# A weight sum made by an adding DMA in a Strassen-Winograd kernel: one core of Trainium2

## Chip, cores and metric

The kernel runs on one core of one Trainium2 chip. The metric is the device time of one launch in microseconds (us). TensorE is called PE, VectorE DVE, ScalarE ACT, GpSimd POOL and SyncE SP, as in the profile.

## What is computed

The reference is a decoder trunk of two layers on a sequence of 512 tokens with 1024 channels. Per layer:

```
x += 0.5 * g1 * SwiGLU1(rms(x) * (1 + s1) + b1)
x += g2 * Mixer(rms(x) * (1 + s2) + b2)
x += 0.5 * g3 * SwiGLU2(rms(x) * (1 + s3) + b3)

def _swiglu(h, w_gate, w_up, w_down):
    return (jax.nn.silu(h @ w_gate) * (h @ w_up)) @ w_down
```

The factors g, s and b come from a conditioning vector `c` by a product with `ada` weights and a bias `ada_b`. The mixer has one input projection, attention with dilated windows, a short convolution, and two gates, sigmoid(g_conv) and sigmoid(g_attn). All data are float32.

## The kernel before

Activations are held transposed, channels on the 128 partitions. Each float32 operand of PE is split into a high part (`hh`, or the first of a pair in `slots_r`, made by ACT as a cast) and a low part (made by DVE as the difference, helper `sub` on L153); a product is three matmuls, high by high, high by low and low by high.

The FFN's gate and up products and the mixer's gate products are made by groups of seven, class `Seven`, by the scheme of Strassen and Winograd. A group takes two weight tiles of 1024 x 256 as `raw1` and `raw2` (gate and up, or two column blocks of `w_in`), each cut into an upper and a lower half of 512 rows: `a`, `c` from the first, `b`, `d` from the second. It multiplies the 2 x 2 blocks of these weights with the 2 x 2 blocks of the activations in seven products of 24 matmuls (128 x 256), with four sums of activation blocks (`Sums.make`, made once per run of groups) and four sums of weight blocks (`minus` on L581, DVE, 128 x 1024 elements each). Product 5 needs b - a, product 6 needs d - b + a, product 7 needs d - b, and product 4 needs c less the operand of product 6. There are 47 groups: 9 in the first FFN, 10 in each of the three others, and 4 in each layer's mixer. `split5` to `split43` prepare the operands, `run56`, `run7` and `run43` issue the matmuls. `kept` (L577) copies a bank to SBUF on ACT, `plus` (L584) adds a bank on DVE.

Weights are loaded by `load` (L202) on SP's queue, in pieces of 512 KB or 1 MB. A scheduler of the framework decides the order of each engine's instructions; every engine takes its own in order. POOL has little to do: a part of the sums of squares of each norm (`Norm.add`, L402), a power for the reciprocal square root (`rstd_of`, L357), and small copies in the attention.

At the kernel's start, `rows` (L280) reads small tables (norm weights, then `ada_b` of each layer) as rows, by DMAs on ACT's queue (L286), and PE transposes them (L291) into `vec`. The first products of the first FFN (L1429) need `hh`, and this needs the conditioning factors and `rs` of the norm, which PE broadcasts (L1386). The four engines share the rest by lines: L548 and L518 are ACT's casts of weight operands and of activation sums, L315 is DVE's product with the `ada` weights.

Of the kernel before, what the change touches and what calls it, by code (L numbers as in the profile page):

```python
# [120 lines left out]
def trunk(ctx: ExitStack, tc: tile.TileContext, x, c, ada_t, ada_b, norm_g, ffn_w_gate, ffn_w_up, ffn_w_down,  # L124
          w_in, conv_w, w_conv_out, w_attn_out, w_o, rel_bias, final_g, buckets, out):
    nc = tc.nc
    V, A, T, G = nc.vector, nc.scalar, nc.tensor, nc.gpsimd
# [3 lines left out]
    sp = ctx.enter_context(tc.tile_pool(name="sp", bufs=2))  # L131
# [20 lines left out]
    def sub(out_, a, b):  # L152
        V.tensor_tensor(out_, a, b, op=ALU.subtract)  # L153
# [42 lines left out]
    def load(*srcs):  # L196

        raw = wp.tile([P, 8, 2 * P], F32, tag="raw", bufs=RAWS, name="raw")
        col = 0
        for s in srcs:  # L200
            kc, n = s.shape[0] // P, s.shape[1]
            nc.sync.dma_start(raw[:, :kc, col:col + n], s.rearrange("(k p) m -> p k m", p=P))  # L202
            col += n
        return raw

    class Unit:

# [28 lines left out]
    def halves_of(raw, kc):  # L236
        return [Unit(raw, kc, 0), Unit(raw, kc, P)]
# [42 lines left out]

    def rows(srcs, col):
        n = sum(s.shape[0] for s in srcs)
        st = sp.tile([P, P], F32, tag="rows", bufs=2, name="rows")
        at = 0
        for s in srcs:
            nc.scalar.dma_start(st[at:at + s.shape[0]], s)  # L286
            at += s.shape[0]

        def end():
            pt = bank("at")  # L290
            T.transpose(pt[:, :n], st[:n], ident[:n, :n])  # L291
            V.tensor_copy(vec[:, col:col + n], pt[:, :n])

        return end
# [204 lines left out]
    class Sums:  # L499
# [11 lines left out]
        def make(self, i, blocks_):  # L511

            h11, h21, h12, h22 = blocks_
            dst, a, b, op = ((h22, h21, h22, ALU.add), (h22, h22, h11, ALU.subtract),
                             (h21, h11, h21, ALU.subtract), (h22, h12, h22, ALU.subtract))[i - 1]
            V.tensor_tensor(dst, a, b, op=op)
            hi, lo = self.parts[i - 1]
            A.copy(hi, dst)  # L518
            sub(lo, dst, f(hi))
# [45 lines left out]
    class Seven:  # L565

        def __init__(self, raw1, raw2, sums, tag="mm"):
            self.a, self.c = raw1[:, :4], raw1[:, 4:]  # L570
            self.b, self.d = raw2[:, :4], raw2[:, 4:]
            self.sums = sums
            self.one, self.two, self.three = bank(tag), bank("at"), None

        def kept(self, src):
            s = F.take()
            A.copy(s.ap, src)  # L577
            return s

        def minus(self, dst, x, y):  # L580
            V.tensor_tensor(dst, x, y, op=ALU.subtract)  # L581

        def plus(self, s, src):
            V.tensor_tensor(s.ap, s.ap, src, op=ALU.add)  # L584
# [11 lines left out]
        def run2(self):  # L596
            self.p2.run()
            self.plus(self.c11, self.two)

        def split5(self, room=None):  # L600
            self.minus(self.a, self.b, self.a)
            self.three = bank("o")
            self.p5 = Product(self.a, self.sums(1), self.three, True, room)

        def split6(self):
            self.minus(self.a, self.d, self.a)
            self.p6 = Product(self.a, self.sums(2), self.one)

        def run56(self):
            self.p5.run()  # L610
            self.p6.run()
            self.c12 = self.kept(self.one)

        def split7(self):
            self.minus(self.b, self.d, self.b)
            self.p7 = Product(self.b, self.sums(3), self.one)

        def run7(self):
# [2 lines left out]
            self.plus(self.c22, self.three)  # L621

        def split43(self):
            self.minus(self.c, self.c, self.a)
            self.p4 = Product(self.c, quarter(1, 1), self.one)
            self.p3 = Product(self.d, self.sums(4), self.three)

# [5 lines left out]
        def out(self):  # L633
            return self.c11, self.c12, self.one, self.c22

    def first_group(raws):

        sums = Sums()
        group = Seven(*raws, sums, "o")
        group.split1()  # L640
        group.split2()
        group.split5(sums.room())
        return group


# [13 lines left out]
    def gate_up(l, i):  # L659

        held = {}

        def raws(m):
            return [load(w[l, i][:, m * P:(m + 2) * P]) for w in (ffn_w_gate, ffn_w_up)]

        def get(m):
            if m not in held:
                g, u = (halves_of(raw, NC) for raw in raws(m))
                held[m], held[m + 1] = (g[0], u[0]), (g[1], u[1])
            return held.pop(m)  # L670

        get.held, get.raws = held, raws
        return get

    def ffn(l, i, get, first, whole):

        acts = {}
        R.top = N_LOW
        group = first_group(get.raws(len(first) + len(first) % 2))

        def swiglu(m, pg, pu):
            t = F.take()
# [8 lines left out]
        def swiglu_pair(m, g1, u1, g2, u2):  # L691

            A.activation(g1.ap, g1.ap, AF.Silu)
            V.tensor_tensor(u1.ap, u1.ap, g1.ap, op=ALU.mult)
            g1.give()
            s = F.take()
            A.activation(s.ap, g2, AF.Silu)
            V.tensor_tensor(u2.ap, u2.ap, s.ap, op=ALU.mult)
            s.give()
            hi, lo = R.take(2), R.take(2)  # L700
            hv, lv = (s.ap.rearrange("p (c n) -> p c n", c=2) for s in (hi, lo))
            for half, t in enumerate((u1, u2)):
                tv = t.ap.rearrange("p (c n) -> p c n", c=2)
                A.copy(hv[:, :, HALF[half]], tv)
                sub(lv[:, :, HALF[half]], tv, f(hv[:, :, HALF[half]]))
                t.give()
            acts[m], acts[m + 1] = zip(hi.apart(), lo.apart())

        wv = whole.ap.rearrange("p (k n) -> p k n", k=NC)
        sums = group.sums  # L710
# [10 lines left out]
        groups = {len(first) + len(first) % 2: group}  # L721
# [6 lines left out]
        def up(part):  # L728
            modulating["phase"] = "up"
            late = None  # L730
            for m in range(*part):
                if m not in groups:
                    continue
                here, after = groups.pop(m), None
                if not begun[0]:
                    make(1)
                    here.split6()
                    make(2)
                    if len(first) % 2 == 0:
                        for n, banks in enumerate(first):  # L740
                            swiglu(n, *banks)
                else:
                    here.split5()
                    here.split6()
                    if late:
                        swiglu_pair(*late)
                if m + 2 < DFF // P:
                    after = groups[m + 2] = Seven(*get.raws(m + 2), sums)
                    after.split1()
                here.run56()  # L750
# [290 lines left out]
    def mixer(l, first):  # L1041
# [123 lines left out]

        def gate_group(col, m):

            return Seven(*(load(w_in[l][:, col + n * P:col + (n + 2) * P]) for n in (m, m + 2)), sums)

        def seven(here, then, make=None):  # L1170

            here.split5(sums.room() if make else None)
            if make:
                make(1)
            here.split6()
            if make:
                make(2)
            if then:
                then.split1()
            here.run56()  # L1180
# [12 lines left out]
            here.run43()  # L1193

            c11, c12, c21, c22 = here.out()
            s = F.take()
            for a, b in ((c11.ap, c11.ap), (s.ap, c21), (c12.ap, c12.ap), (c22.ap, c22.ap)):
                A.activation(a, b, AF.Sigmoid)
            return [(c11, s), (c12, c22)]

        def begin(group):
# [17 lines left out]
        sums = Sums(False)  # L1219
# [20 lines left out]
        here = begin(gate_group(C_GC, 0))  # L1240
# [300 lines left out]
```

## Time and profile before

| | us |
|---|---|
| median of 3 runs | 2647.26 (2643.28 to 2652.77) |
| profiled execution | 2646.32 |
| its span, first to last instruction | 2644.5 |
| PE busy | 2599.9 |
| DVE busy | 1936.0 |
| ACT busy | 1215.4 |
| POOL busy | 207.6 |

The time is that of one core. An engine's busy time counts its own instructions, and an engine waits when an operand, a free buffer or a bank is not there; the profile names what ended each wait. Engines overlap, so the sums of their busy times exceed the span.

### The profile page before, as it was taken

Reading aid. Unit: us, or ns where it says so; the run is one execution under the profiler, and the core shown is the slowest. Engines: PE = TensorE matmul, PEld = TensorE weight load, DVE = VectorE, ACT = ScalarE, POOL = GpSimd, SP = SyncE. Lnnn points to the kernel's source line nnn. Section 1 sums busy time; section 2 is a strip of 40 time slices with the busy share of each in tenths; the row PEclk is TensorE's granted clock in tenths of the full one; section 3 lists DMA queues with packets and bytes.
Section 4 is the critical chain, followed back from the end, with each engine's and each line's share of the span. In section 5 each row is a group of like instructions: output and inputs, shape, how many; then the busy total and the mean of one; then the engine's idle time right before and its main releaser. Section 6 shows DMA issues by size and latency. Waiting matters only on the chain.

```text
span 2644.5 us, 41896 instructions
## 1 busy us (share of the span) xinstructions
PE 2599.9 (98%) x16841; PEld 2362.5 (89%) x16841; DVE 1936.0 (73%) x2971; ACT 1215.4 (46%) x2224; POOL 207.6 (8%) x545
## 2 busy tenths in 40 slices
PE   8999999999999999999999999999999999999998
PEld 6899999888888989999999999988898888999998
DVE  8987775674685778888788777666756957777675
ACT  5454454353353455444554445443344435545443
POOL 0000031011010020000020000321111000200001
PEclk9999999999999999999999999999999999999999
DMA  9543253352323134353424424343433223233321
GB/s 328 191 161 121 67 156 122 113 166 88 120 88 128 62 130 139 133 191 112 144 73 159 152 96 129 118 130 104 151 112 104 96 96 128 65 112 105 104 77 68
DMA packets 285487, 326.52 MB, mean 123 GB/s; under 512 B 8057, under 2 KB 263404, under 8 KB 285292
## 3 DMA queue, kind: packets, MB, share of 16 engines
q1 hardware_dynamic: 284980, 323.71, 37.5%
q8 instruction: 132, 2.16, 0.3%
q14 instruction: 63, 0.52, 0.1%
q10 hardware_dynamic: 312, 0.13, 0.0%
HBM read 321.67 MB, written 2.13 MB: 122 GB/s over the span
## 4 chain that ended last, share of the span: by engine, by line
PE 66%; DVE 2%; ACT 1%; DMA 1%; POOL 0%; issue 0%; POOLq 0%; ACTq 0%; DVEq 0%; SPq 0%
PE mm L559 14%; PE o L559 9%; PE mm L243 8%; PE mm L244 8%; PE mm L245 8%; PE at L559 4%; PE o L243 2%; PE o L245 2%; PE o L244 2%; PE mm L1130 2%; PE at L245 2%; PE at L244 2%; PE at L243 2%; DVE slots_r L153 1%; PE o L967 1%
## 5 line engine op out<-in xcount | busy, mean ns | idle before, releaser
L153 DVE TENSOR_TENSOR slots_r<-raw,slots_r 128x1024 fp32r<-128x1024 f32 (+3 forms) x457 | 447.6, 999 | 148.6 <-ACT slots_r L548 91.7
L548 ACT CAST slots_r<-raw 128x1024 fp32r<-128x1024 f32 x329 | 341.0, 1049 | 445.7 <-DVE raw L581 71.1
L223 DVE TENSOR_TENSOR slots_r<-raw,slots_r 128x512 fp32r<-128x512 f32 (+3 forms) x520 | 320.7, 638 | 211.4 <-ACT slots_r L222 77.2
L222 ACT CAST slots_r<-raw 128x512 fp32r<-128x512 f32 (+3 forms) x520 | 289.7, 577 | 381.5 <-PE mm L245 106.0
L243 PE MATMUL mm<-hh,slots_r 128*128 128x512 f32 (+1 forms) x1064 | 385.2, 365 | 0.0
L244 PE MATMUL mm<-hl,slots_r 128*128 128x512 f32 (+1 forms) x1064 | 383.3, 361 | 0.3 <-DVE hl L153 0.3
L245 PE MATMUL mm<-hh,slots_r 128*128 128x512 f32 (+1 forms) x1064 | 382.6, 360 | 0.0
L559 PE MATMUL o<-slots_r 128*128 128x256 f32 x2448 | 310.6, 285 | 6.1 <-ACT slots_r L518 3.1
L559 PEld LDWEIGHTS o<-slots_r 128*128 128x128 f32 x2448 | 302.6, 193 | 8.2 <-ACT slots_r L518 3.7
L559 PE MATMUL mm<-slots_r 128*128 128x256 f32 x2064 | 264.8, 284 | 2.5 <-ACT slots_r L548 0.9
L559 PE MATMUL mm<-hh,slots_r 128*128 128x256 f32 x1376 | 258.5, 280 | 5.9 <-ACT slots_f L577 5.9
L559 PEld LDWEIGHTS mm<-slots_r 128*128 128x128 f32 x2064 | 255.5, 193 | 5.6 <-ACT slots_f L577 3.1
L581 DVE TENSOR_TENSOR raw<-raw 128x1024 f32<-128x1024 f32 x188 | 230.0, 1226 | 3.9 <-DMA raw<-in_w_in_dram 0.6
L245 PEld LDWEIGHTS mm<-hh,slots_r 128*128 128x128 f32 x1064 | 201.3, 189 | 32.2
L244 PEld LDWEIGHTS mm<-hl,slots_r 128*128 128x128 f32 x1064 | 201.8, 190 | 26.6 <-DVE hl L153 0.6
L559 PEld LDWEIGHTS mm<-hh,slots_r 128*128 128x128 f32 x1376 | 216.4, 188 | 9.4 <-ACT slots_f L577 9.1
L243 PEld LDWEIGHTS mm<-hh,slots_r 128*128 128x128 f32 x1064 | 200.5, 190 | 26.5 <-ACT hh L377 0.2
L244 PE MATMUL mm<-slots_r 128*128 128x512 f32 (+1 forms) x584 | 212.3, 364 | 0.0
L243 PE MATMUL mm<-slots_r 128*128 128x512 f32 (+1 forms) x584 | 212.3, 365 | 0.0
L245 PE MATMUL mm<-slots_r 128*128 128x512 f32 (+1 forms) x584 | 212.2, 363 | 0.0
L559 PE MATMUL mm<-hl,slots_r 128*128 128x256 f32 x688 | 192.0, 279 | 0.0
L559 PE MATMUL at<-hh,slots_r 128*128 128x256 f32 x752 | 141.4, 280 | 0.9 <-DVE slots_r L153 0.9
(197 smaller groups left out, 4598.1 us busy)
## 6 DMA issues: line engine op xcount, KB each, us to landing
slots_f<-in_ada_t_dram SPq DMA_DIRECT2D x144, 512.0 KB, 4.7
raw<-in_w_in_dram SPq DMA_DIRECT2D x52, 1024.0 KB, 5.1
raw<-in_ffn_w_gate_dram SPq DMA_DIRECT2D x42, 1024.0 KB, 5.2
raw<-in_ffn_w_up_dram SPq DMA_DIRECT2D x42, 1024.0 KB, 5.7
raw<-in_ffn_w_down_dram SPq DMA_DIRECT2D x32, 768.0 KB, 4.8
raw<-in_w_in_dram SPq DMA_DIRECT2D x48, 512.0 KB, 5.1
raw<-in_ffn_w_down_dram SPq DMA_DIRECT2D x20, 512.0 KB, 3.4
raw<-in_w_conv_out_dram SPq DMA_DIRECT2D x8, 1024.0 KB, 7.4
```

The costliest lines, as they stand in the source:

```text
L153: V.tensor_tensor(out_, a, b, op=ALU.subtract)
L222: A.copy(hv, src)
L223: (eng or V).tensor_tensor(lv, src, f(hv), op=ALU.subtract)
L243: T.matmul(dst, hi, xh[:, cols], start=first, stop=False)
L244: T.matmul(dst, hi, xl[:, cols], start=False, stop=False)
L245: T.matmul(dst, lo, xh[:, cols], start=False, stop=last)
L548: A.copy(hv, src)
L559: T.matmul(dst, a, b, start=self.first and k == i == n == 0, stop=True, skip_group_check=True)
L581: V.tensor_tensor(dst, x, y, op=ALU.subtract)
L967: T.matmul(dst, a, b, start=first[bk], stop=True, skip_group_check=True)
L1130: T.matmul(dst, a, b, start=k == 0 and r % 2 == 0 and n == 0, stop=True, skip_group_check=True)
```

## The change

Quarter `b` of the second weight tile gets `d` added by a DMA from POOL's queue, which reads the same half of the weights again and adds it to what the load put there. Products take the derived sums with changed signs: `a += b` is the operand of product 6, then `c += a` that of product 4, then `a -= d` that of product 5, and b itself that of product 7. Product 6 is made and run ahead of product 5. The changed signs are taken back in `Sums.make`, in `swiglu_pair` and in the scale of a sigmoid. The tile of `rows` gets one buffer where it had two, and a scratch area for DMAs 4096 bytes where it had 1024.

```diff
-        st = sp.tile([P, P], F32, tag="rows", bufs=2, name="rows")
+        st = sp.tile([P, P], F32, tag="rows", bufs=1, name="rows")
...
-            dst, a, b, op = ((h22, h21, h22, ALU.add), (h22, h22, h11, ALU.subtract),
-                             (h21, h11, h21, ALU.subtract), (h22, h12, h22, ALU.subtract))[i - 1]
-            V.tensor_tensor(dst, a, b, op=op)
+            dst, a, b = ((h22, h22, h21), (h22, h22, h11), (h21, h11, h21), (h22, h22, h12))[i - 1]
+            if i % 2:
+                sub(dst, a, b)
+            else:
+                V.scalar_tensor_tensor(dst, a, -1.0, b, op0=ALU.mult, op1=ALU.subtract)
...
-        def __init__(self, raw1, raw2, sums, tag="mm"):
+        def __init__(self, srcs, sums, tag="mm"):
+
+            raw1, raw2 = (load(s) for s in srcs)
             self.a, self.c = raw1[:, :4], raw1[:, 4:]
             self.b, self.d = raw2[:, :4], raw2[:, 4:]
+            G.dma_start(self.b, srcs[1][D // 2:].rearrange("(k p) m -> p k m", p=P), accum_op=ALU.add)
...
+        def split6(self, room=None):
+            V.tensor_tensor(self.a, self.a, self.b, op=ALU.add)
+            self.p6 = Product(self.a, self.sums(2), self.one, room=room)
+
         def split5(self, room=None):
-            self.minus(self.a, self.b, self.a)
+            V.tensor_tensor(self.c, self.c, self.a, op=ALU.add)
+            sub(self.a, self.a, self.d)
             self.three = bank("o")
             self.p5 = Product(self.a, self.sums(1), self.three, True, room)
 
-        def split6(self):
-            self.minus(self.a, self.d, self.a)
-            self.p6 = Product(self.a, self.sums(2), self.one)
-
-        def run56(self):
-            self.p5.run()
+        def run6(self):
             self.p6.run()
             self.c12 = self.kept(self.one)
 
+        def run5(self):
+            self.p5.run()
+
         def split7(self):
-            self.minus(self.b, self.d, self.b)
             self.p7 = Product(self.b, self.sums(3), self.one)
...
         def split43(self):
-            self.minus(self.c, self.c, self.a)
...
-            V.tensor_tensor(u1.ap, u1.ap, g1.ap, op=ALU.mult)
+            V.scalar_tensor_tensor(u1.ap, u1.ap, -1.0, g1.ap, op0=ALU.mult, op1=ALU.mult)
...
-    nc = bacc.Bacc("TRN2", target_bir_lowering=False, num_devices=1, dynamic_dma_scratch_size=1024)
+    nc = bacc.Bacc("TRN2", target_bir_lowering=False, num_devices=1, dynamic_dma_scratch_size=4096)
```

`split5` and `split6` change places in `ffn`, in `first_group` and in the mixer's `seven`, and `run6` and `run5` follow each other there. In the changed file the lines stand 1 to 7 further down (L286 is L287, L1429 is L1436, the adding DMA is L578).

The first pair of orders is that of ACT at the kernel's start; `rows` is the small table's tile, `in_ada_b_dram` the bias, `slots_f<-slots_f` the activation of `c`. Before:

```order
L286 DMA rows<-in_final_g_dram 8x128
L286 DMA rows<-in_ada_b_dram 72x128
L1367 ACTIVATE hl,ssq<-slots_f 128x1024 x4
L1383 ACTIVATE slots_f<-slots_f 128x1024
L286 DMA rows<-in_ada_b_dram 72x128
L1376 COPY xT<-mm 128x4x128 x4
L1388 COPY slots_f<-at 128x512
```

After:

```order
L287 DMA rows<-in_final_g_dram 8x128
L1374 ACTIVATE hl,ssq<-slots_f 128x1024 x4
L1390 ACTIVATE slots_f<-slots_f 128x1024
L287 DMA rows<-in_ada_b_dram 72x128
L1383 COPY xT<-mm 128x4x128 x4
L287 DMA rows<-in_ada_b_dram 72x128
L1395 COPY slots_f<-at 128x512
```

Both transfers of `ada_b` have moved down, the first behind the five activations, the second behind the four copies.

The second pair is that of DVE at the first group of the mixer's gates in layer 0. `raw_6908` and `raw_6910` are the group's weight tiles; L516 and L519 are `make`, and L153 or L154 with `slots_r` is the lower part of an operand, of a weight block where `raw` is read and of an activation sum where `slots_f` is. Before:

```order
L581 TENSOR_TENSOR raw_6908<-raw_6910,raw_6908 128x1024
L584 TENSOR_TENSOR slots_f_70<-slots_f_70,at_6913 128x512
L516 TENSOR_TENSOR slots_f_70<-slots_f_70 128x1024
L153 TENSOR_TENSOR slots_r_69<-raw_6908,slots_r_69 128x1024
L516 TENSOR_TENSOR slots_f_70<-slots_f_70 128x1024
L153 TENSOR_TENSOR slots_r_69<-raw_6910,slots_r_69 128x1024
L153 TENSOR_TENSOR slots_r_69<-slots_f_70,slots_r_69 128x1024 x2
```

After:

```order
L609 TENSOR_TENSOR raw_6908<-raw_6908 128x1024
L588 TENSOR_TENSOR slots_f_70<-slots_f_70,at_6914 128x512
L154 TENSOR_TENSOR slots_f_70<-slots_f_70 128x1024
L154 TENSOR_TENSOR raw_6908<-raw_6908,raw_6910 128x1024
L154 TENSOR_TENSOR slots_f_70<-slots_f_70 128x1024
L154 TENSOR_TENSOR slots_r_69<-slots_f_70,slots_r_69 128x1024
L154 TENSOR_TENSOR slots_r_69<-raw_6908,slots_r_69 128x1024
L519 SCALAR_TENSOR_TENSOR slots_f_70<-slots_f_70 128x1024
```

The lower parts of product 5's sum and weight have moved ahead of `make(2)`, and one `make` (that of product 7) too.

The third pair is that of POOL from the last attention head of layer 0 to the norm of the second FFN. Before:

```order
L813 COPY ng_6496<-top 32x2 x16
L813 COPY sm0x<-sm_6529 32x2 x16
L402 TENSOR_TENSOR slots_f<-slots_f 128x256 x5
L357 TENSOR_TENSOR rs<-rs,minus_half 128x2
L402 TENSOR_TENSOR slots_f<-slots_f 128x256 x5
```

After:

```order
L819 COPY ng_6496<-top 32x2 x16
L578 DMA raw<-in_w_in_dram 128x4x256
L819 COPY sm0x<-sm_6529 32x2 x16
L578 DMA raw<-in_w_in_dram 128x4x256 x3
L578 DMA raw<-in_ffn_w_up_dram 128x4x256
L403 TENSOR_TENSOR slots_f<-slots_f 128x256 x3
L578 DMA raw<-in_ffn_w_up_dram 128x4x256
L403 TENSOR_TENSOR slots_f<-slots_f 128x256 x2
L358 TENSOR_TENSOR rs<-rs,minus_half 128x2
L403 TENSOR_TENSOR slots_f<-slots_f 128x256 x5
```

Six adding DMAs now stand between POOL's instructions here, one of them within the first five sums of squares.

## Rows read from the trace of the kernel before

**Rows 1.** The page: the span, and PE's busy time, share and instructions.

```profile
span 2644.5 us, 41896 instructions
PE 2599.9 (98%) x16841; PEld 2362.5 (89%) x16841; DVE 1936.0 (73%) x2971; ACT 1215.4 (46%) x2224; POOL 207.6 (8%) x545
```

**Rows 2.** Who waited for whom, PE: us in total, times, longest.

```profile
PE mm L559 <- ACT slots_f L577: 6.6, 5, 1.7
PE at L411 <- POOL slots_f L402: 3.7, 2, 1.9
```

**Rows 3.** Groups of DVE by form: busy us, mean ns | idle before, releasers.

```profile
L581 DVE TENSOR_TENSOR raw<-raw 128x1024 f32<-128x1024 f32 x188 | 230.0, 1226 | 3.9 <-DMA raw<-in_w_in_dram 0.6
...
L388 DVE SCALAR_TENSOR_TENSOR xT<-mm,mod,xT 128x512 f32<-128x512 f32 x72 | 52.1, 744 | 14.1 <-PE mm L245 14.1
...
L694 DVE TENSOR_TENSOR slots_f<-slots_f 128x512 f32<-128x512 f32 x39 | 26.8, 687 | 0.6
```

**Rows 4.** Timeline of DVE in the second FFN: start, duration, instruction, [idle before, releaser].

```profile
1095.99 2.49 DVE L581 TENSOR_TENSOR raw<-raw 128x1024 f32<-128x1024 f32 x2
1098.39 0.68 DVE L584 TENSOR_TENSOR slots_f<-slots_f,o 128x512 f32<-128x512 f32 x1
...
1117.62 1.23 DVE L153 TENSOR_TENSOR slots_r<-raw,slots_r 128x1024 fp32r<-128x1024 f32 x1 [3.70 <-ACT slots_r L548]
```

**Rows 5.** Timeline of PE there: product 3, then the next group's product 5.

```profile
1122.07 5.93 PE L559 MATMUL o<-slots_r 128*128 128x256 f32 x48
```

**Rows 6.** DMA issues: count, KB each, median us from issue to landing.

```profile
raw<-in_w_in_dram SPq DMA_DIRECT2D x48, 512.0 KB, 5.1
raw<-in_ffn_w_down_dram SPq DMA_DIRECT2D x20, 512.0 KB, 3.4
```

**Rows 7.** Timeline of ACT at the start.

```profile
11.13 0.32 ACTq L286 DMA_DIRECT2D rows<-in_ada_b_dram  x1
```

**Rows 8.** Timeline of PE at the start.

```profile
14.78 1.06 PE L1386 MATMUL at<-ident,rs 128*128 128x128 f32 x4
17.57 0.38 PE L291 MATMUL at<-ident,rows 72*128 72x72 f32 x1 [1.72 <-DMA rows<-in_ada_b_dram]
18.27 2.01 PE L1429 MATMUL mm<-hh,slots_r 128*128 128x512 f32 x3 [0.32 <-ACT hh L1401]
...
24.55 0.50 PE L1429 MATMUL o<-hh,slots_r 128*128 128x512 f32 x1 [0.96 <-DVE slots_r L223]
```

**Rows 9.** Stretches: length, busy us (instructions) of PE, PEld, DVE, ACT, POOL; clock; DMA.

```profile
18.00:92.00 74.00, 68.77 (x363) 57.38 (x364) 73.60 (x116) 39.48 (x56) 0.00 (x0) 0.97 0.71 249
...
791.50:796.80 5.30, 5.27 (x24) 5.28 (x25) 5.30 (x6) 1.08 (x2) 0.00 (x0) 0.50 0.01 3
...
2096.00:2103.00 7.00, 5.35 (x26) 4.76 (x27) 7.00 (x9) 2.19 (x4) 0.00 (x0) 0.76 0.00 0
```

**Rows 10.** Timeline of PE at the first mixer group of layer 0.

```profile
789.21 0.38 PE L559 MATMUL o<-slots_r 128*128 128x256 f32 x1 [1.85 <-ACT slots_r L518]
791.53 5.28 PE L559 MATMUL o<-slots_r 128*128 128x256 f32 x23 [1.93 <-DVE slots_r L153]
...
806.75 0.50 PE L559 MATMUL o<-slots_r 128*128 128x256 f32 x2 [1.02 <-ACT slots_r L548]
```

**Rows 11.** SP's timeline in the stretch from 960 to 975 us, the last load.

```profile
963.38 0.37 SPq L202 DMA_DIRECT2D raw<-in_ffn_w_up_dram  x1
```

**Rows 12.** DMA issues of that stretch: the same load, us to landing.

```profile
raw<-in_ffn_w_up_dram SPq DMA_DIRECT2D x1, 1024.0 KB, 7.2
```

**Rows 13.** Timeline of POOL at the norm of the second FFN.

```profile
969.24 3.19 POOL L402 TENSOR_TENSOR slots_f<-slots_f 128x256 f32<-128x256 f32 x4 [2.07 <-ACT slots_f L399]
974.67 0.71 POOL L357 TENSOR_TENSOR rs<-rs,minus_half 128x2 f32<-128x2 f32 x1 [2.24 <-DVE rs L356]
...
977.83 0.74 POOL L402 TENSOR_TENSOR slots_f<-slots_f 128x256 f32<-128x256 f32 x1 [1.57 <-ACT slots_f L399]
```

**Rows 14.** Timeline of PE there.

```profile
982.08 0.39 PE L244 MATMUL mm<-hl,slots_r 128*128 128x256 f32 x1 [0.35 <-DVE hl L153]
```

More of the change, by code (lines that the diff above doesn't have):

```diff
@@ L578, in kept @@
             return s
-        def minus(self, dst, x, y):
-            V.tensor_tensor(dst, x, y, op=ALU.subtract)
         def plus(self, s, src):
@@ L634, in out, with first_group @@
             return self.c11, self.c12, self.one, self.c22
-    def first_group(raws):
+    def first_group(srcs):
         sums = Sums()
-        group = Seven(*raws, sums, "o")
+        group = Seven(srcs, sums, "o")
         group.split1()
         group.split2()
-        group.split5(sums.room())
+        group.split6(sums.room())
         return group
@@ L661, in gate_up, with srcs @@
         held = {}
-        def raws(m):
-            return [load(w[l, i][:, m * P:(m + 2) * P]) for w in (ffn_w_gate, ffn_w_up)]
+        def srcs(m):
+            return [w[l, i][:, m * P:(m + 2) * P] for w in (ffn_w_gate, ffn_w_up)]
         def get(m):
             if m not in held:
-                g, u = (halves_of(raw, NC) for raw in raws(m))
+                g, u = (halves_of(load(s), NC) for s in srcs(m))
                 held[m], held[m + 1] = (g[0], u[0]), (g[1], u[1])
             return held.pop(m)
-        get.held, get.raws = held, raws
+        get.held, get.srcs = held, srcs
         return get
@@ L678, in ffn @@
         R.top = N_LOW
-        group = first_group(get.raws(len(first) + len(first) % 2))
+        group = first_group(get.srcs(len(first) + len(first) % 2))
         def swiglu(m, pg, pu):
@@ L697, in swiglu_pair @@
             A.activation(s.ap, g2, AF.Silu)
-            V.tensor_tensor(u2.ap, u2.ap, s.ap, op=ALU.mult)
+            V.scalar_tensor_tensor(u2.ap, u2.ap, -1.0, s.ap, op0=ALU.mult, op1=ALU.mult)
             s.give()
@@ L736, in up @@
                     make(1)
-                    here.split6()
+                    here.split5()
                     make(2)
@@ L742, in up @@
                 else:
+                    here.split6()
                     here.split5()
-                    here.split6()
                     if late:
@@ L747, in up @@
                 if m + 2 < DFF // P:
-                    after = groups[m + 2] = Seven(*get.raws(m + 2), sums)
+                    after = groups[m + 2] = Seven(get.srcs(m + 2), sums)
                     after.split1()
-                here.run56()
+                here.run6()
+                here.run5()
                 make(3)
@@ L1166, in gate_group @@
         def gate_group(col, m):
-            return Seven(*(load(w_in[l][:, col + n * P:col + (n + 2) * P]) for n in (m, m + 2)), sums)
+            return Seven([w_in[l][:, col + n * P:col + (n + 2) * P] for n in (m, m + 2)], sums)
         def seven(here, then, make=None):
-            here.split5(sums.room() if make else None)
+            here.split6(sums.room() if make else None)
             if make:
                 make(1)
-            here.split6()
+            here.split5()
             if make:
@@ L1179, in seven @@
                 then.split1()
-            here.run56()
+            here.run6()
+            here.run5()
             if make:
@@ L1196, in seven @@
             s = F.take()
-            for a, b in ((c11.ap, c11.ap), (s.ap, c21), (c12.ap, c12.ap), (c22.ap, c22.ap)):
-                A.activation(a, b, AF.Sigmoid)
+            for a, b, sign in ((c11.ap, c11.ap, 1.0), (s.ap, c21, 1.0), (c12.ap, c12.ap, -1.0), (c22.ap, c22.ap, -1.0)):
+                A.activation(a, b, AF.Sigmoid, scale=sign)
             return [(c11, s), (c12, c22)]
```

## The prediction

> **What bounds the kernel now.** I read the page's totals first, then the waits of TensorE (PE), then the stretches where these waits lie. PE is busy for 2599.9 of 2644.5 us [rows 1]: all its gaps together are 44.6 us, and that is the most that any change can win which leaves PE's matmuls as they are. This one does: every group still has seven products of 24 matmuls, in the order 6, 5, 7 where it was 5, 6, 7. VectorE (DVE), which loses work, is no bound over the whole, so what counts is where PE waits for it. The largest waits tell where [rows 2]. Those for the copy on L577 are 6.6 us, nearly all of them one wait of about 1.6 us in the last group of each FFN, where product 4 needs the bank that `kept` still copies; product 7, that copy and product 4 follow each other as before, so they stay. The waits for GpSimd's (POOL) sums of squares are 3.7 us. The rest lies at the kernel's start and at the first group of each run of groups, and is shown below.
>
> **DVE's work.** Four subtractions of 1.226 us per group become three additions or subtractions of the same tile size, so 47 of the 188 go: 47 x 1.226 = 57.6 us [rows 3]. The signs turn some TENSOR_TENSORs into SCALAR_TENSOR_TENSORs; at 512 columns the one form is 0.687 us (L694) and the other 0.744 (L388, which also reads a bank), so 0 to 0.06 us each, on some 80 of 512 columns and 12 of 1024, that is 0 to 6 us of DVE time. Neither is on PE's path inside a run of groups. There DVE works far ahead: its first subtractions on a new group start at 1095.99 [rows 4], by when both weight tiles have landed, and PE reaches the group's product 5 only in the second half of the 48 matmuls from 1122.07 [rows 5], at 1122.07 + 5.93 / 2 = 1125. What covers DVE is thus some 29 us of earlier products, and taking 1.2 us out of that lead is worth **0**.
>
> **The accumulating DMA.** No such transfer is in the trace. It moves 512 KB. Loads of this size from SyncE (SP) land 3.4 and 5.1 us after issue [rows 6]; below I can't go under 3.4, and above I allow 14: twice the 5.1, for reading the destination too, and some 4 for POOL's issue, which no row prices. I take 6, near the plain load. Its wait for the load holds nothing in a run of groups but the next such DMA. Behind it stands `a += b`. In the changed order that addition comes after the addition onto `c22` that starts at 1098.39 and takes 0.68 [rows 4], so at least 3 us of the transfer are hidden before DVE notices, and a blocked DVE then eats into the lead of 29 us; DVE also has slack to catch up, such as the 3.70 us before 1117.62 [rows 4]. I take a third of that lead as free (10 us), a choice, since DVE has the other work of two groups to do in it; then PE stalls only if the transfer takes over 3 + 10 = **13 us** from the load's landing. At 6 us: 0. The Trainium skill, "DMA: Bandwidth & Descriptors", section "Anatomy of one DMA", fits a transfer issued from GpSimd with 2.0 us plus the bytes at 436 GB/s, which makes an estimate of 3.2 us here; by it the sum is the same.
>
> **The kernel's start.** `rows` gets one buffer where it had two, and this I price highest. Before, the first `ada_b` transfer is issued with the other small ones, and only the second at 11.13 [rows 7]; it lands at 17.57, 6.4 us later, in a stretch where loads fill the queue, and PE's transposition of it ends just before the first product (18.27) [rows 8]. After (the first pair of order fences), the first `ada_b` transfer has to wait for PE's transposition of the earlier rows and stands behind the activation of `c`: it is issued at about 11.1 and lands at about 17.6. PE transposes it ahead of the broadcast of `rs` (14.78 before), so everything that hangs on that, `hh` above all, comes 17.95 - 14.78 = 3.2 us later: 18.27 + 3.2 = 21.4. The second can be issued only at about 18.0, and by the same 6.4 us lands at 24.4, and its transposition stands ahead of the first product: PE starts at 24.5 and not at 18.27, 6.2 us late. Some comes back, for PE waited later for DVE and ScalarE (ACT) too (0.96 us before 24.55 [rows 8], and later again), and these are only 3.2 us late. From 18 to 92 us DVE is busy 73.60 of 74.00 us [rows 9]; it is the bound of that stretch, so its 3.2 us reach the end of it whole, less 0.5 for the first group (one 1024-column operation less, one of 512 more ahead of its last sums). The bounds are 0 (the small transfer lands early) and +6.2; I take **+3.5**. In the same stretch the first group's accumulate runs while loads fill the queue: **+0.5**, bounds -1 and +4.
>
> **The first groups of the mixers.** PE waits 1.85 and 1.93 us at 789 and 791 and 1.02 us at 806.75 [rows 10]; at 791.5 the granted clock is 0.50 for 5.3 us, the lower of the two levels (1.2 GHz), in which 24 matmuls take 5.3 us where 24 take 3.0 at 2.4 GHz [rows 5, 9]. So this start costs 2.0 + 1.9 + 2.3 + 1.0 = some 7 us, and that of layer 1 (PE busy 5.35 of 7 us at a clock of 0.76 [rows 9]) 1.7 of waits and as much of clock. DVE decides both. Ahead of the first products one 1.2-us subtraction is gone, and the lower half of the sums of product 5 now comes ahead of `make(2)` (second pair of fences): the second matmul of product 5 can start about 1.1 us earlier, and the later waits shrink by 1 to 2 us. The clock still falls, because PE still waits some 3 us. I take -2.5 and -0.5, together **-3**; bounds -12 (waits and clock all gone) and +1.
>
> **POOL's queue.** Two accumulates stand ahead of or among the sums of squares of each later norm (third pair of fences), and in a queue in order the sums wait for a weight load and the issue. The load that the second one waits for is issued at 963.38 [rows 11] and takes 7.2 us to land [rows 12], at 970.6. POOL's sums run from 969.24, the power at 974.67 [rows 13]: two of them can come some 1 to 2 us later, and the power with them. The sums behind wait for ACT anyway (1.57 us before 977.83 [rows 13]), which takes the delay up. PE waits 0.35 us for `hl` at 982.08 [rows 14], so there is hardly slack. Three such places, 0 to +1.7 each: **+2**, bounds 0 and +5.
>
> **Sum.** 0 + 3.5 + 0.5 - 3 + 2 = +3 on the profiled execution's 2646.3 us (its span of 2644.5 and 1.8 around it), which is 0.9 below the median of the runs: 2649.
>
> **The rivals.** (1) *Nothing shows*: the small transfers at the start land soon and POOL's delays are taken up; what is left is the mixers' -3: 2643 to 2647. For it speaks that every term is small; against, that the row on the load of `ada_b` gives 6.4 us in just that stretch. (2) *Faster*: DVE's relief at the mixers' starts is enough that PE doesn't fall to the lower clock, -12, and the start costs at most +2: 2636. Against it: the table load and casts of ACT are ahead of the same products, and they stay. (3) *Slower by the starts*: all of +6.2, +4 and +5 and no gain at the mixers: 2646 + 15 = 2661. (4) *Slower by the accumulate*: from 13 us on it decides; at 15 each of some 35 groups inside a run loses 2 us: 2646 + 70 = 2716. For it: the transfer has to read its destination too, and no row bounds its issue on POOL; against: DVE's lead. The Trainium skill, "SBUF — State Buffer", section "two separate sides", has a rule that speaks for it: descriptors of a DMA issued on GpSimd are written through a port pair that DVE can lock, and one such DMA went from 0.62 to 3.1 us beside a copy. Times five, 6 us would be 30, and every group would lose 17; but it names copies in a two-port mode, and DVE here does additions and subtractions. No row here shows either. (5) *The change does not do what it says*: the subtractions go as counted, that is sure from the order; it is only the time that can miss.
>
> **Chances.** My forecast (2647 to 2654) 0.45, rival 1 0.20, rival 2 0.11, rival 3 0.16, rival 4 0.08. Measurement tells 0.3%, 7.9 us, from no change: the first two are "same", 0.65; faster 0.11; slower 0.24. The range leaves out rival 4 and most of rival 2: 2639 to 2663.
>
> **What would show it.** Right: 141 operations on the three new lines in DVE; PE's first product at about 24 us; no new waits inside the runs of groups; PE's sum of gaps within 10 us of 44.6; POOL's power near 976. Wrong: waits of PE or DVE for a DMA from GpSimd's queue in every group; a first product still at 18; a clock of 1.0 at the mixers' start.

## The result, and the profile after

The changed kernel takes 2685.1 us, median of 4 runs (2678.7 to 2695.9), beside 2649.8 for the kernel before (4 runs): a ratio of 1.0135, with a 95% interval of 1.0114 to 1.0157. It is 35 us slower where I forecast no measurable change.

The page of the kernel after, span and busy times:

```profile
span 2685.9 us, 42026 instructions
PE 2612.6 (97%) x16841; PEld 2372.1 (88%) x16841; DVE 1881.1 (70%) x2924; ACT 1209.2 (45%) x2224; POOL 267.1 (10%) x592
```

Against [rows 1] DVE has 54.9 us less work, about what was counted, and PE has the same 16841 matmuls. PE's gaps are now 2685.9 - 2612.6 = 73.3 us where they were 44.6, which is 28.7 us more. The other 12.7 us of the 41.4 us by which the span grew are PE's own: the same matmuls are busy longer. The mean granted clock of the run is 0.989 where it was 0.993, so some 0.011 x 2685.9 = 29.5 us are lost to the clock where 18.5 were: 11 of the 12.7. One such fall stands right behind a wait of 3.66 us that is shown below (stretch: length, busy us of PE, PEld, DVE, ACT, POOL; clock; DMA):

```profile
1342.00:1348.00 6.00, 6.00 (x29) 6.00 (x29) 1.62 (x6) 1.71 (x4) 1.44 (x2) 0.50 0.00 0
```

At this place the kernel before had a clock of 0.75 for 6 us. So a gap can be paid partly a second time, in the matmuls behind it.

Who waited for whom on PE, after (us in total, times, longest):

```profile
PE mm L562 <- ACT slots_f L584: 9.8, 9, 2.5
PE at L412 <- POOL slots_f L403: 9.3, 5, 3.7
PE at L292 <- DMA rows<-in_ada_b_dram: 7.7, 2, 5.1
PE o L562 <- DVE slots_f L588: 7.1, 6, 2.1
...
PE o L562 <- ACT slots_r L551: 4.6, 4, 2.2
```

No releaser in this list is the adding DMA. The two rows of [rows 2] have grown to 9.8 and 9.3 us, and the third row, the small table at the start, is new in its size. The DMA shows one engine further back. First DVE's groups by form (busy us, mean ns | idle before, releasers), then the adding DMA's issues in the FFNs (min/median/max ns on POOL, first and last start), and the us to landing of all 47:

```profile
L605 DVE TENSOR_TENSOR raw<-raw 128x1024 f32<-128x1024 f32 x47 | 57.5, 1224 | 75.9 <-issue 36.6 <-DMA raw<-in_ffn_w_up_dram 33.0 <-DMA raw<-in_w_in_dram 3.1
L154 DVE TENSOR_TENSOR raw<-raw 128x1024 f32<-128x1024 f32 x47 | 57.5, 1223 | 1.0
L609 DVE TENSOR_TENSOR raw<-raw 128x1024 f32<-128x1024 f32 x47 | 57.5, 1223 | 0.7
```

```profile
L578 POOL DMA_DIRECT2D raw<-in_ffn_w_up_dram x39: 1273/1288/1465, 60.1 to 2589.0; - x39
...
DMA to landing us min/median/max: 5.6/5.8/9.2
```

DVE stands 75.9 us in all before the 47 additions `a += b` (L605), and hardly at all before the other two of each group (1.7 us). The profile names no releaser for 36.6 of the 75.9 us (`issue`). The landings tell: in 26 of the 47 groups the addition starts 0.08 us after its adding DMA has landed, and these groups have some 73 of the 75.9 us. The transfer itself is what I had assumed: 5.8 us, and 1.29 us of POOL for its issue.

**Where the time goes.** From the start of the matmul with the same number in each trace I worked out how far a kernel lags the kernel before (us; negative is ahead):

| place (time before) | after | e2 | e6 | e8 | e3 |
|---|---|---|---|---|---|
| 214.5, first FFN | 8.4 | 4.3 | 1.9 | 2.2 | 0.1 |
| 811.7, mixer of layer 0 | 7.0 | 1.3 | 2.4 | -1.7 | -3.2 |
| 1258.0, second FFN | 13.6 | 3.4 | 2.5 | -0.6 | -4.5 |
| 1341.6, third FFN begun | 21.6 | 5.6 | 3.0 | 6.7 | -5.5 |
| 1421.3, its `w_down` begun | 29.6 | 6.5 | 6.6 | 8.3 | -3.8 |
| end | 41.0 | 5.7 | 9.5 | 14.2 | -4.5 |

The loss comes in steps. The two largest, of 7 to 8 us, lie where one kind of work passes into another; the others are of 1 to 4 us. The two, in the rows of the kernel after:

*Second FFN to third.* DVE's timeline (start, duration, instruction, [idle before, releaser]), then POOL's and PE's:

```profile
1321.99 1.22 DVE L154 TENSOR_TENSOR slots_r<-raw,slots_r 128x1024 fp32r<-128x1024 f32 x1
1331.40 1.23 DVE L605 TENSOR_TENSOR raw<-raw 128x1024 f32<-128x1024 f32 x1 [8.20 <-issue]
1332.54 0.75 DVE L389 SCALAR_TENSOR_TENSOR xT<-mm,mod,xT 128x512 f32<-128x512 f32 x1
```

```profile
1322.11 1.29 POOL L578 DMA_DIRECT2D raw<-in_ffn_w_up_dram  x1 [61.22 <-DVE xT L389]
...
1337.66 3.93 POOL L403 TENSOR_TENSOR slots_f<-slots_f 128x256 f32<-128x256 f32 x5 [5.22 <-ACT slots_f L400]
```

```profile
1333.43 0.36 PE L244 MATMUL mm<-slots_r 128*128 128x256 f32 x1 [1.60 <-DVE xT L389]
1341.64 2.72 PE L412 MATMUL at<-ones,slots_f 128*128 128x1 f32 x12 [3.66 <-POOL slots_f L403]
```

The adding DMA of the third FFN's first group is issued at 1322.11 and lands 9.2 us later, at 1331.3, the longest of all (SP had issued two weight loads at 1320.50 and 1320.96). DVE has come to `a += b` at 1323.20 and stands until 1331.40. The operand of that addition is needed only after the next norm. But behind it in DVE's queue stand the residual additions of the second FFN (L389), and they are needed at once: by PE for a bank, by ACT and POOL for the next norm, and by PE for its sums. PE's waits of 1.60 and 3.66 us name DVE and POOL, and the cause is a DMA two engines away.

*Last group of the third FFN to `w_down`.* POOL, DVE, SP, ACT and PE, one row or two each, with the same columns:

```profile
1400.35 1.33 POOL L578 DMA_DIRECT2D raw<-in_ffn_w_up_dram  x1 [31.14 <-DMA raw<-in_ffn_w_up_dram]
...
1406.35 1.23 DVE L605 TENSOR_TENSOR raw<-raw 128x1024 f32<-128x1024 f32 x1 [4.26 <-DMA raw<-in_ffn_w_up_dram]
...
1415.27 8.38 SPq L203 DMA_DIRECT2D raw<-in_ffn_w_down_dram  x3
...
1420.05 1.44 ACT L223 CAST slots_r<-raw 128x512 fp32r<-128x512 f32 x3 [5.26 <-DMA raw<-in_ffn_w_down_dram]
1421.40 0.57 ACT L584 COPY slots_f<-mm 128x512 f32<-128x512 f32 x1
...
1422.02 0.39 PE L562 MATMUL mm<-hh,slots_r 128*128 128x256 f32 x1 [2.15 <-ACT slots_f L584]
```

The same loads on SP's queue in the kernel before:

```profile
1389.04 7.56 SPq L202 DMA_DIRECT2D raw<-in_ffn_w_down_dram  x3
```

The lag at this place, at 1377.1 of before, is 22.0 us, so the `w_down` loads would go at 1411.0. They go at 1415.27, 4.2 us later, when DVE has read the group's weight tiles for the last time (L154, from 1414.03 to 1415.25). DVE has stood 4.26 us at the addition that these readings stand behind. ACT's cast then waits 5.26 us for one of these loads, the copy `kept` (L584) stands behind the cast, and PE waits 2.15 us for the copy.

### The profile page after: what moved, and what is told of

Same layout as the page of the kernel before. It is cut to its first block, busy times and chain, and to the rows that moved or that the text cites. A ratio compares the mean times of both kernels' runs of the same rounds, so it can differ in the third digit from the quotient of the medians.

```text
span 2685.9 us, 42026 instructions
## 1 busy us (share of the span) xinstructions
PE 2612.6 (97%) x16841; PEld 2372.1 (88%) x16841; DVE 1881.1 (70%) x2924; ACT 1209.2 (45%) x2224; POOL 267.1 (10%) x592
## 4 chain that ended last, share of the span: by engine, by line
PE 74%; DVE 11%; DMA 8%; ACT 3%; issue 3%; POOL 1%; SPq 0%; POOLq 0%; DVEq 0%; ACTq 0%
PE mm L562 12%; PE mm L245 11%; PE mm L244 11%; PE mm L246 10%; PE o L562 8%; DMA raw<-in_ffn_w_up_dram 4%; DVE slots_r L154 4%; PE mm L1136 3%; PE at L562 2%; PE o L244 2%; PE o L246 2%; PE o L245 2%; DMA raw<-in_ffn_w_down_dram 2%; PE at L246 2%; PE at L245 2%
## 5 line engine op out<-in xcount | busy, mean ns | idle before, releaser
L154 DVE TENSOR_TENSOR slots_r<-raw,slots_r 128x1024 fp32r<-128x1024 f32 (+3 forms) x457 | 446.9, 1003 | 161.9 <-ACT slots_r L551 97.4
L562 PE MATMUL o<-slots_r 128*128 128x256 f32 x2448 | 320.4, 288 | 14.1 <-DVE slots_f L588 7.1
L562 PEld LDWEIGHTS mm<-hh,slots_r 128*128 128x128 f32 x1376 | 217.2, 189 | 14.4 <-ACT slots_f L584 13.2
L578 POOL DMA_DIRECT2D raw<-in_ffn_w_up_dram x39 | 50.5, 1296 | 1302.4 <-DMA raw<-in_ffn_w_up_dram 663.2
```

Source lines behind the costliest of these rows:

```text
L562: T.matmul(dst, a, b, start=self.first and k == i == n == 0, stop=True, skip_group_check=True)
L578: G.dma_start(self.b, srcs[1][D // 2:].rearrange("(k p) m -> p k m", p=P), accum_op=ALU.add)
```

## The experiments

**e2: nobody waits soon for the sum.** `a` gets `d` and not `b` added, so products 6, 4 and 5 take other sums. The DMA stays, and its first reader is the split of product 7.

```diff
-            V.tensor_tensor(self.a, self.a, self.b, op=ALU.add)
+            V.tensor_tensor(self.a, self.a, self.d, op=ALU.add)
```

> The changed kernel with a += d in the place of a += b: DVE's operation has the same size and place, but d is there with the load, so it need not wait for the adding DMA; the DMA still runs, and its sum is first read by product 7. Product 6 and what is derived from it get another weight sum than the reference's. Theory A: 22 to 32 us faster than the changed kernel, at most 10 us above before. Rival B: within 5 us of the changed kernel, since queue and traffic are the same. Rival C: the same as the changed kernel.

Measured: 2655.8 us, 1.0022 [1.0013, 1.0032]. Same DMAs, same number of DVE operations, and 30 of the 36 us (1.0135) are gone. DVE's row in e2 and PE's waits:

```profile
L605 DVE TENSOR_TENSOR raw<-raw 128x1024 f32<-128x1024 f32 x47 | 57.4, 1221 | 1.3 <-DMA raw<-in_ffn_w_up_dram 0.5
```

```profile
PE at L292 <- DMA rows<-in_ada_b_dram: 8.3, 2, 5.4
PE at L412 <- POOL slots_f L403: 7.6, 5, 1.9
...
PE mm L562 <- ACT slots_f L584: 1.3, 3, 0.6
```

So it is the wait at `a += b` that costs these 30 us, not the transfer's traffic or its issue.

**e3: the same order and signs, the sum on DVE.** No adding DMA; `rows` has its two buffers and the scratch area its 1024 bytes again.

```diff
-            G.dma_start(self.b, srcs[1][D // 2:].rearrange("(k p) m -> p k m", p=P), accum_op=ALU.add)
...
+            V.tensor_tensor(self.b, self.b, self.d, op=ALU.add)
```

> No adding DMA: b += d is made on DVE, so each group has four DVE operations as before, but in the order and with the signs of the changed kernel; rows with two buffers and the scratch area of before. Theory A: within 5 us of before (2645 to 2655), or a few us faster. Rival C: still 15 us or more slower than before. Rival B: near before too.

Measured: 2643.8 us, 0.9977 [0.9968, 0.9987]: faster than both kernels. DVE does the 57.7 us of additions that the change had removed, and waits less:

```profile
L604 DVE TENSOR_TENSOR raw<-raw 128x1024 f32<-128x1024 f32 x47 | 57.7, 1228 | 22.6 <-DMA raw<-in_ffn_w_up_dram 11.9 <-DMA raw<-in_w_in_dram 10.7
```

DVE's addition waits for the load alone (22.6 us); through the DMA the same sum is there about 6.5 us after the load (0.7 to the issue, 5.8 to landing) where DVE makes it in 1.2.

**e4: the kernel before with one buffer for `rows`.**

```diff
-        st = sp.tile([P, P], F32, tag="rows", bufs=2, name="rows")
+        st = sp.tile([P, P], F32, tag="rows", bufs=1, name="rows")
```

> The kernel before with one buffer for rows, nothing else. All theories but D: 3 to 6 us slower than before, PE's first product at 24 us and not at 18. Rival D: 25 us or more slower. If the late transfer is hidden: no difference.

Measured: 2648.4 us, 0.9996 [0.9986, 1.0005]. PE's timeline at its start:

```profile
22.92 0.35 PE L291 MATMUL at<-ident,rows 72*128 72x72 f32 x1 [5.50 <-DMA rows<-in_ada_b_dram]
23.02 2.91 PE L1429 MATMUL mm<-hh,slots_r 128*128 128x512 f32 x6
```

The first product is 4.75 us later than in [rows 8], as foreseen, and the time does not show it.

**e5: the changed kernel with two buffers for `rows`**, the scratch area at 2048 bytes, since two buffers and 4096 bytes (e1) don't fit together in SBUF.

```diff
-        st = sp.tile([P, P], F32, tag="rows", bufs=1, name="rows")
+        st = sp.tile([P, P], F32, tag="rows", bufs=2, name="rows")
...
-    nc = bacc.Bacc("TRN2", target_bir_lowering=False, num_devices=1, dynamic_dma_scratch_size=4096)
+    nc = bacc.Bacc("TRN2", target_bir_lowering=False, num_devices=1, dynamic_dma_scratch_size=2048)
```

> The changed kernel with two buffers for rows, the scratch area cut to 2048 bytes so that both fit. Theory A, with the one buffer worth little: within 5 us of the changed kernel (2685), PE's first product back at 18 us. If the start, though nothing in the kernel before, counts where DVE is later anyway: 4 to 8 us faster than the changed kernel. Rival E (the scratch area sets the pace of the adding DMA): slower than the changed kernel.

Measured: 2681.4 us, 1.0127 [1.0112, 1.0142], which overlaps the 1.0135 of the change, with PE's first product back at 18.26. The start is not where the 35 us are. Nor does the smaller scratch area slow the adding DMA: its median to landing is 5.8 us as before.

**e6: the tile that gets the sum is loaded first.** Loads of a group change places, nothing else.

```diff
-            raw1, raw2 = (load(s) for s in srcs)
+            raw2, raw1 = (load(s) for s in srcs[::-1])
```

> The changed kernel with the order of each group's two loads turned round: the tile that is added to is loaded first, so the adding DMA runs while the other tile is loaded. Theory A: DVE's waits at a += b, 73 us in the changed kernel, fall under 20 us, and the time by 20 to 30 us, to 2655 to 2665. Rival B (queue and traffic): within 5 us of the changed kernel.

Measured: 2655.3 us, 1.0019 [1.0008, 1.0031]. The adding DMA now runs beside the load of the other tile, and L605 waits 6.2 us in all:

```profile
L605 DVE TENSOR_TENSOR raw<-raw 128x1024 f32<-128x1024 f32 x47 | 57.4, 1220 | 6.2 <-DMA raw<-in_ffn_w_up_dram 3.6 <-issue 1.2 <-DVE slots_r L154 0.6
```

So the wait can be taken away with the DMA kept.

**e7: e6 with e5's two edits**, the tile loaded first and two buffers for `rows`.

```diff
+            raw2, raw1 = (load(s) for s in srcs[::-1])
...
+        st = sp.tile([P, P], F32, tag="rows", bufs=2, name="rows")
...
+    nc = bacc.Bacc("TRN2", target_bir_lowering=False, num_devices=1, dynamic_dma_scratch_size=2048)
```

> As the run with the turned loads, and two buffers for rows with 2048 bytes of scratch. Theory A: 0 to 4 us faster than the turned loads alone; 2645 to 2662. It is the version that could be as fast as the sum made on DVE (2644) if nothing of the DMA is left on the path.

Measured: 2652.8 us, 1.0018 [1.0008, 1.0027]: no difference from e6 that shows.

**e8: half the sum.** The DMA adds 256 KB into the first two of the four blocks of `b`; the other two get no sum.

```diff
-            G.dma_start(self.b, srcs[1][D // 2:].rearrange("(k p) m -> p k m", p=P), accum_op=ALU.add)
+            G.dma_start(self.b[:, :2], srcs[1][D // 2:D // 2 + 2 * P].rearrange("(k p) m -> p k m", p=P), accum_op=ALU.add)
```

> The changed kernel with an adding DMA of half the rows (256 KB; the lower two of four blocks of b get no sum). Theory A: the DMA lands some 1 to 2 us sooner, each of some 23 waits at a += b is shorter by that, and the time falls by 8 to 16 us, to 2669 to 2677. Rival C (order and signs): the same as the changed kernel. Rival B: some 5 us faster.

Measured: 2661.5 us, 1.0047 [1.0031, 1.0063]. DVE's row, and the landing:

```profile
L605 DVE TENSOR_TENSOR raw<-raw 128x1024 f32<-128x1024 f32 x47 | 57.4, 1222 | 48.3 <-DMA raw<-in_ffn_w_up_dram 28.4 <-issue 17.1 <-DMA raw<-in_w_in_dram 1.9
...
DMA to landing us min/median/max: 4.1/4.4/8.1
```

A landing 1.4 us sooner takes DVE's waits from 75.9 to 48.3, but wins 24 of the 36 us. The loss isn't in proportion to the wait. A reading that fits, though no run here isolates it: what costs is what is left of each wait over the slack of what stands behind it.

**e9: `a += b` on POOL**, so that DVE does not stand there.

```diff
-            V.tensor_tensor(self.a, self.a, self.b, op=ALU.add)
+            G.tensor_tensor(self.a, self.a, self.b, op=ALU.add)
```

> The changed kernel with a += b made on POOL, behind the adding DMA in POOL's own queue: DVE no longer stands still there, but the operand of product 6 comes as late as before or some us later, and the weight tiles are held as long. Theory A1 (what costs is DVE's queue behind the wait): 15 to 29 us faster than the changed kernel, 2656 to 2670. Theory A2 (what costs is that the operand and the tile's release are late, whichever engine waits): within 8 us of the changed kernel or slower.

Measured: 2688.6 us, 1.0145 [1.0125, 1.0165]. This run does not tell what it was made for, since DVE still stands. It waits 34.0 us in all at `a -= d` (L609), which needs POOL's sum, and at the boundary shown above residual additions stand behind it again:

```profile
1340.24 1.23 DVE L609 TENSOR_TENSOR raw<-raw 128x1024 f32<-128x1024 f32 x1 [6.71 <-POOL raw L605]
1341.38 3.22 DVE L389 SCALAR_TENSOR_TENSOR xT<-mm,mod,xT 128x256 f32<-128x256 f32 x8
```

The lag grows by 8.1 us there (1294.9 to 1341.6 of before). POOL's addition takes 2.56 us, and the norms' sums of squares stand behind it too:

```profile
L605 POOL TENSOR_TENSOR raw<-raw 128x1024 f32<-128x1024 f32 x47 | 120.3, 2561 | 257.7 <-DVE slots_r L154 119.6 <-DMA raw<-in_ffn_w_up_dram 65.8 <-DVE slots_f L588 27.7
```

The wait moved to another queue in order, its operand came later than from DVE, and DVE stood for it one addition further on. How much of the 30 us is DVE's queue, and how much the late operand and the weight tile that comes free late, this run leaves open.

**e10: e3 with e6's edit.**

```diff
+            raw2, raw1 = (load(s) for s in srcs[::-1])
...
+            V.tensor_tensor(self.b, self.b, self.d, op=ALU.add)
```

> The kernel with the sum on DVE and the new order, with the two loads of a group turned round. DVE waits there 22 us in all for the second tile; turned round, b += d can run before the first tile is there, but a += b needs both, so the waits move rather than go: within 4 us of the run with the sum on DVE (0.9977 of before).

Measured: 2644.6 us, 0.9983 [0.9972, 0.9993]. Without the DMA the order of the loads is worth nothing. Against e7, which differs only by who makes the sum and the scratch area, the DMA still costs 0.0035 of 2650, some 9 us, with hardly a wait of DVE for it.

**e11: the order of products alone.** The signs of before, in the sums of activations and the activations behind them too; all four weight sums on DVE; product 6 first; `rows` and the scratch area as before.

```diff
-            G.dma_start(self.b, srcs[1][D // 2:].rearrange("(k p) m -> p k m", p=P), accum_op=ALU.add)
...
+            sub(self.b, self.d, self.b)
...
-            V.tensor_tensor(self.c, self.c, self.a, op=ALU.add)
-            sub(self.a, self.a, self.d)
+            sub(self.c, self.c, self.a)
+            sub(self.a, self.d, self.a)
```

> The kernel before with the new order alone (product 6 first, the four subtractions b = d - b, a += b, c -= a, a = d - a on DVE, all signs as before, no SCALAR_TENSOR_TENSOR). If the order is what made the sum on DVE faster than before: 4 to 9 us faster than before (0.9966 to 0.9985). If the signs or another part did: the same as before.

Measured: 2643.7 us, 0.998 [0.9968, 0.9992], as e3: the signs cost nothing, and the gain is that of the order. PE's waits of e11:

```profile
PE at L412 <- POOL slots_f L403: 3.7, 2, 1.9
...
PE mm L560 <- ACT slots_f L581: 1.6, 3, 0.7
```

The 6.6 us of [rows 2] for the copy of a bank are 1.6.

**e12: in the first group of each FFN the sum is made by DVE**, by the DMA in the other 43 groups.

```diff
+            if not self.acc:
+                V.tensor_tensor(self.b, self.b, self.d, op=ALU.add)
...
-        group = Seven(srcs, sums, "o")
+        group = Seven(srcs, sums, "o", acc=False)
```

> The changed kernel with the sum b += d made on DVE in the first group of each FFN (4 of the 47), by the adding DMA in the others. Theory A, with what stands behind the wait on DVE as the price: at the step from one FFN to the next the residual's additions stand behind it and the changed kernel loses 7 us at one such step, so 6 to 12 us faster than the changed kernel (2673 to 2679). If every wait costs alike, 4 of 47: 3 us faster.

Measured: 2678.6 us, 1.0119 [1.0095, 1.0142]. At the boundary shown above DVE goes through:

```profile
1320.75 1.22 DVE L608 TENSOR_TENSOR raw<-raw 128x1024 f32<-128x1024 f32 x1
1322.00 1.23 DVE L609 TENSOR_TENSOR raw<-raw 128x1024 f32<-128x1024 f32 x1
1323.14 0.74 DVE L389 SCALAR_TENSOR_TENSOR xT<-mm,mod,xT 128x512 f32<-128x512 f32 x1
```

The lag there goes from 11.9 to 12.3 us, where it went from 13.6 to 21.6: that step is this wait's. But `a += b` (L609 here) still waits 64.9 us in all. By the ratios the time is only some 4 us better, by the medians 6.5, and the intervals overlap: the four first groups are the smaller part of the loss, the other 43 the larger.

**e13: the DMA in the 8 mixer groups alone**, on DVE elsewhere, with e12's `if` and `acc` off but in the mixer.

```diff
-            return Seven([w_in[l][:, col + n * P:col + (n + 2) * P] for n in (m, m + 2)], sums)
+            return Seven([w_in[l][:, col + n * P:col + (n + 2) * P] for n in (m, m + 2)], sums, acc=True)
```

> The adding DMA in the 8 groups of the mixers alone, the 39 of the FFNs with the sum on DVE. DVE waits 3 us of 76 at a += b in the mixers, so theory A: 25 us or more faster than the changed kernel, within 5 us of the run with every sum on DVE (2639 to 2650).

Measured: 2649.8 us, 1.0001 [0.999, 1.0011], 6 us behind e3. It has e3's order but the change's single buffer for `rows` and its scratch area, so these 6 us lie with eight DMAs, the start and that area together.

## Why the prediction was wrong

**The step that failed** is the one on the adding DMA: "I take a third of that lead as free (10 us), a choice", and from it "PE stalls only if the transfer takes over 3 + 10 = 13 us". The transfer took 5.8 us from issue and some 6.5 from the load's landing, near the 6 that I took, and by that threshold cost 0. It cost 30 us, the difference of e2 and the change (1.0135 - 1.0022 = 0.0113 of 2650). By e8 most of the loss is gone where the sum lands some 5.1 us after the load (0.7 and 4.4), so the threshold lies nearer 5 than 13. What was wrong with it: the 29 us were read for one operand, product 5's weight sum, in the middle of a run. A wait of DVE holds back all that stands behind it, and what stands there has leads of its own. At the two steps shown it was a residual addition that PE needed for a bank and the norm for its sums, and a group whose end lets the `w_down` loads start. That is rival 4's mechanism from a point less than half as far as I put it, and at the ends of runs where I had looked inside them. e2, e6 and e8 show the wait to be the cause. The two steps show it as well when DVE's wait there is set beside the growth of the lag (us):

| | after | e8 | e12 | e6 | e2 |
|---|---|---|---|---|---|
| second FFN to third: DVE's wait | 8.20 | 6.59 | 0 | 0.46 | 0 |
| lag, 1258.0 to 1341.6 | +8.0 | +7.3 | +0.4 | +0.5 | +2.2 |
| to `w_down`: DVE's wait | 4.26 | 1.23 | 2.90 | 1.92 | 0 |
| lag, 1341.6 to 1421.3 | +8.0 | +1.6 | +3.9 | +3.6 | +0.9 |

The waits are those of `a += b`, at the first place in e8 and at the second in e8, e12 and e6:

```profile
1314.98 1.23 DVE L605 TENSOR_TENSOR raw<-raw 128x1024 f32<-128x1024 f32 x1 [6.59 <-issue]
...
1388.41 1.23 DVE L605 TENSOR_TENSOR raw<-raw 128x1024 f32<-128x1024 f32 x1 [1.23 <-DMA raw<-in_ffn_w_up_dram]
...
1395.67 1.23 DVE L609 TENSOR_TENSOR raw<-raw 128x1024 f32<-128x1024 f32 x1 [2.90 <-DMA raw<-in_ffn_w_up_dram]
...
1385.42 1.22 DVE L605 TENSOR_TENSOR raw<-raw 128x1024 f32<-128x1024 f32 x1 [1.92 <-DMA raw<-in_ffn_w_up_dram]
```

At each place the runs with the longer waits lose more, from one trace of each run; the 2.2 us of e2 without a wait show what else can move there.

**The transfer itself** was right. The Trainium skill, "DMA: Bandwidth & Descriptors", section "Anatomy of one DMA", gave an estimate of 3.2 us for it; measured are 5.8, and 4.4 for half the bytes, so 1.4 us for 256 KB and some 3.0 fixed. Here the measurement decides, and the page's figure would have hidden the wait even more. The rule of the Trainium skill, "SBUF — State Buffer", section "two separate sides", that I weighed for rival 4 does not show: with DVE busy 70% the median is 5.8, the shortest 5.6, and POOL's issues take 1.29 us.

**DVE's work**: 47 operations of 1.22 us fewer, worth nothing on PE's path. Right, and e3 makes it plain: giving the operations back costs no time.

**The start**: the mechanism came as described, PE's first product is at 23.42 (forecast 24.5), the two waits 2.61 and 5.06 us:

```profile
17.02 0.38 PE L292 MATMUL at<-ident,rows 72*128 72x72 f32 x1 [2.61 <-DMA rows<-in_ada_b_dram]
17.19 1.06 PE L1393 MATMUL at<-ident,rs 128*128 128x128 f32 x4
23.32 0.35 PE L292 MATMUL at<-ident,rows 72*128 72x72 f32 x1 [5.06 <-DMA rows<-in_ada_b_dram]
23.42 2.91 PE L1436 MATMUL mm<-hh,slots_r 128*128 128x512 f32 x6
```

Its +3.5 is the term that I priced highest and that can't be seen: e4 lies between -3.7 and +1.3 us, e5 and e7 show none. I had DVE bound to the end of that stretch. In e4's trace the kernel is 1.6 us behind at 92 us and level at 811.7: what is lost at the start is made up later, where is not shown. The first group's own DMA, +0.5 forecast with bounds -1 and +4: at 92 us the kernel after is 4.1 us behind and e12, which makes that sum on DVE, 1.4, so some 2.7 by one trace each.

**The mixers**: -3 forecast. Around the first groups of layer 0 the lag falls by 2.8 us after the change and by 3.3 in e3, so this is not the DMA's doing. For layer 1 I forecast -0.5: from 2080 to 2135 us of before the lag goes from 37.1 to 37.2, so nothing was won. The clock does fall, as I said: the changed kernel's stretch in layer 0:

```profile
798.00:806.00 8.00, 6.47 (x29) 5.98 (x30) 8.00 (x8) 4.33 (x6) 0.00 (x0) 0.57 0.01 2
```

**POOL's queue**: +2 forecast, bounds 0 and +5. PE's waits for POOL's sums are 9.3 us, but in e2, where DVE doesn't stand, 7.6, against 3.7 before: +3.9, within the bounds. In e11, without the DMAs, they are 3.7 again.

**The order of products** I put at nothing: "product 7, that copy and product 4 follow each other as before, so they stay". They did not stay: the 6.6 us fall to 1.6 (e11). The 6.6 us are in the main four waits of 1.26 to 1.66 us, and only two of these lie in the last group of an FFN, as the prediction has it; the others lie in that of a mixer. ACT's rows at the first of the four, two of the kernel before and two of e11:

```profile
339.75 0.62 ACT L222 CAST slots_r<-raw 128x512 fp32r<-128x512 f32 x1 [1.17 <-DMA raw<-in_w_in_dram]
340.28 0.58 ACT L577 COPY slots_f<-mm 128x512 f32<-128x512 f32 x1
...
337.80 0.58 ACT L581 COPY slots_f<-mm 128x512 f32<-128x512 f32 x1
339.08 2.08 ACT L223 CAST slots_r<-raw 128x512 fp32r<-128x512 f32 x4 [0.71 <-DMA raw<-in_w_in_dram]
```

On PE product 4 still follows product 7. But on ACT the copy of product 7's bank stood behind a weight cast that waited for a load, and in e11 it stands ahead of that cast; product 4 waits 0.54 us for it where it waited 1.56. The whole gain of the order is 5 us by e11's ratio and 6 by e3's. Other waits move both ways too, so that it is this one alone is not shown.

**The account**, in ratios: the order -0.002 (e11), the DMA without the wait +0.0042 (e2 less e11, 11 us, with the signs, the one buffer and the scratch area), the wait +0.0113 (30 us): together +0.0135, as they must, since each is the difference of two neighbours in a chain of runs. Of the 11 us the norms' 3.9 are seen; e13's 6 us lie in eight DMAs, the start and the scratch area; how the rest divides stays open.

## What to carry to other kernels

An engine that takes its instructions in order passes a wait on to everything behind it: before a wait is put down to a lead, read the lead of each of the next instructions in its queue, at the ends of runs above all, and not that of the operand alone. To move an operation of 1.2 us from an engine with slack to a transfer that comes 6.5 us after the load, as here, shortens a sum of busy times and lengthens a path; if it must be, the tile that gets the sum is loaded first. And where a change has several parts, take the one that wins alone: here the order of two products, 5 us, without the DMA.

## What the runs showed that I had not expected

The adding DMA costs some 3.0 us and 1.4 us for each 256 KB (187 GB/s), beside 1.20 to 1.29 us of POOL for each issue, and the one issued 1.2 us after the second of two weight loads took 9.2 us. POOL adds two 128 x 1024 tiles in 2.56 us where DVE takes 1.22. A lag grows in steps: at 1294.9, 1341.6, 1377.1 and 1421.3 us of before the kernel after is 14.4, 21.6, 22.0 and 29.6 us behind, so it loses 7 to 8 us at each of the two places shown and 0.4 in the 36 us between them.
